# Two parity stores at the end of a row-normalizing kernel, and unshared buffers for its row sums

## Chip, cores, metric

One core of a Trainium2 chip. The metric is the device time of one execution in microseconds (us); medians of several executions are given.

## The reference

```python
x: [32, 512, 1024] float32          # 64 MiB in, 64 MiB out
sums = np.sum(np.abs(x), axis=-1, keepdims=True)
return (x / (sums + 1e-8)).astype(np.float32)
```

Each row of 1024 numbers is divided by the sum of its magnitudes. There is little arithmetic per byte: 134.22 MB cross between HBM and SBUF.

## The kernel before

The 16384 rows are cut into eleven tiles: ten of 12 rows per partition (6 MB), one of 8 (4 MB). Each tile is loaded by the SP queue, reduced and scaled in place by VectorE (DVE), with one row in twelve (five in the first tile, none at the end) left to ScalarE (ACT), and stored by the ACT queue. Four tile buffers rotate.

```python
    rows = [R] * ((per_partition - HEAD) // R + 2) + [HEAD - 2 * R]   # ten times 12, then 8
    sbuf = ctx.enter_context(tc.tile_pool(name="sbuf", bufs=BUFS))    # BUFS = 4
    stats = ctx.enter_context(tc.tile_pool(name="stats", bufs=4))
    # ... normalize():
        s = stats.tile([P, R], FP32)
        nc.vector.tensor_reduce(out=s[:, :k], in_=x_tile[...], ..., apply_absolute_value=True)
        nc.vector.tensor_scalar_add(out=s[:, :k], in0=s[:, :k], scalar1=EPS)
        inv = stats.tile([P, R], FP32)
        nc.vector.reciprocal(out=inv[:, :k], in_=s[:, :k])
        nc.vector.tensor_mul(out=x_tile[...], in0=x_tile[...], in1=inv[...])   # rows 0..kv
        # ... rows kv..k: nc.scalar.activation(Copy, scale=inv[:, r : r + 1])
    # ... the loop over the tiles:
            x_tile = sbuf.tile([P, R, d], FP32)
            nc.sync.dma_start(out=x_tile[:, :k, :], in_=piece(x_flat, i))
            normalize(...)
            nc.scalar.dma_start(out=piece(out_flat, i), in_=x_tile[:, :k, :])
```

## Time and profile before

| | before |
|---|---|
| median of the first 3 executions | 316.74 us (316.55 to 316.98) |
| span of the profiled execution (its time) | 317.3 us (318.93 us) |
| DVE busy | 268.7 us |
| DMA packets, bytes | 3168, 134.22 MB |

### The profile page before, as it was taken

The page shows a single profiled execution, that of the slowest core. Times are in us where ns is not written, and L with a number is a line of the kernel's source. Part 1 is how long each engine was busy: PE and PEld are TensorE (multiplying, and loading weights), DVE is VectorE, ACT ScalarE, POOL GpSimd, SP SyncE. Part 2 cuts the span into 40 slices and gives each one's busy share as a digit, 9 for nine tenths or more (in the row PEclk, how much of TensorE's full clock was granted, in tenths as well). Part 3 has the DMA queues.
Part 4 walks back from the last instruction along what each step waited for, and adds up shares of the span by engine and source line. Part 5 has one row for each costly group of instructions (what it writes and reads, how often), then busy time and mean ns, then how long its engine had stood idle before and what let it go on. Part 6 is the DMA issues. An engine that isn't in the chain of part 4 may idle for free.

```text
span 317.3 us, 170 instructions
## 1 busy us (share of the span) xinstructions
DVE 268.7 (85%) x44; ACT 13.5 (4%) x12; POOL 0.2 (0%) x4
## 2 busy tenths in 40 slices
DVE  0079999999999999989995996799699969999920
ACT  0010601001000000100100010000000000000000
POOL 0000000000000000000000000000000000000000
DMA  8999999999999999999999999999999999999994
GB/s 328 465 397 471 421 378 415 415 465 409 459 434 397 477 415 415 465 409 459 428 403 477 409 428 452 409 471 415 403 477 415 428 430 452 397 477 415 403 425 215
DMA packets 3168, 134.22 MB, mean 423 GB/s; under 512 B 352, under 2 KB 352, under 8 KB 352
## 3 DMA queue, kind: packets, MB, share of 16 engines
q1 hardware_dynamic: 1584, 67.11, 49.6%
q10 hardware_dynamic: 1584, 67.11, 48.9%
HBM read 67.11 MB, written 67.11 MB: 423 GB/s over the span
## 4 chain that ended last, share of the span: by engine, by line
DVE 52%; DMA 34%; another core or an unknown queue 9%; issue 0%; SPq 0%; DVEq 0%; ACTq 0%
DVE s L51 27%; DVE x_tile L61 24%; DMA x_tile<-in_x_dram 18%; DMA out_dram<-x_tile 16%; DVE inv L60 1%; DVE s L58 0%; SPq L78 0%; DVEq L60 0%; ACTq L85 0%
## 5 line engine op out<-in xcount | busy, mean ns | idle before, releaser
L51 DVE TENSOR_REDUCE s<-x_tile 128x12 f32<-128x12288 f32 (+1 forms) x11 | 138.2, 12561 | 32.9 <-DMA x_tile<-in_x_dram 32.9
L61 DVE TENSOR_TENSOR x_tile<-x_tile,inv 128x11264 f32<-128x11264 f32 (+3 forms) x11 | 126.5, 11504 | 0.4
L68 ACT ACTIVATE x_tile<-x_tile,inv 128x1024 f32<-128x1024 f32 x11 | 12.2, 1142 | 153.6 <-DVE inv L60 153.6
L60 DVE RECIPROCAL inv<-s 128x12 f32<-128x12 f32 (+1 forms) x11 | 2.5, 226 | 0.9
L58 DVE TENSOR_SCALAR s<-s 128x12 f32<-128x12 f32 (+1 forms) x11 | 1.9, 173 | 0.4
L68 ACT ACT_TABLE_LOAD x1 | 1.3, 1283 | 17.8 <-DMA x_tile<-in_x_dram 17.8
L100 POOL MEMSET const-bfloat16-1.0<- 128x1 bf16 x1 | 0.1, 102 | 0.0
L100 POOL MEMSET const-uint8-127<- 128x1 uint8 x1 | 0.1, 102 | 0.0
L100 POOL MEMSET const-float32-0.0<- 128x1 f32 x1 | 0.1, 99 | 0.2 <-issue 0.2
L100 POOL MEMSET const-float32-1.0<- 128x1 f32 x1 | 0.1, 99 | 0.0
## 6 DMA issues: line engine op xcount, KB each, us to landing
x_tile<-in_x_dram SPq DMA_DIRECT2D x10, 6144.0 KB, 39.2
out_dram<-x_tile ACTq DMA_DIRECT2D x10, 6144.0 KB, 43.7
x_tile<-in_x_dram SPq DMA_DIRECT2D x1, 4096.0 KB, 35.4
out_dram<-x_tile ACTq DMA_DIRECT2D x1, 4096.0 KB, 13.0
```

Of the source, the lines that this page charges most:

```text
L51: nc.vector.tensor_reduce(out=s[:, :k], in_=x_tile[:, r0 : r0 + k, :], axis=mybir.AxisListType.X, op=mybir.AluOpType.add, apply_absolute_v ...
L58: nc.vector.tensor_scalar_add(out=s[:, :k], in0=s[:, :k], scalar1=EPS)
L60: nc.vector.reciprocal(out=inv[:, :k], in_=s[:, :k])
L61: nc.vector.tensor_mul(out=x_tile[:, r0 : r0 + kv, :], in0=x_tile[:, r0 : r0 + kv, :], in1=inv[:, :kv].unsqueeze(2).to_broadcast([P, kv, d]),)
L68: nc.scalar.activation(out=row, in_=row, func=mybir.ActivationFunctionType.Copy, scale=inv[:, r : r + 1],)
L100: nc = _bacc.Bacc("TRN2", target_bir_lowering=False, num_devices=1)
```

## The change

Its intent, as far as it shows: finish the tail in smaller stores, and let no tile wait for the row sums of an earlier one.

```diff
-    stats = ctx.enter_context(tc.tile_pool(name="stats", bufs=4))
+    stats = ctx.enter_context(tc.tile_pool(name="stats", bufs=len(rows)))
...
-            nc.scalar.dma_start(out=piece(out_flat, i), in_=x_tile[:, :k, :])
+
+            parts = 1 if i + 2 < len(rows) else 2
+            for j in range(parts):
+                nc.scalar.dma_start(
+                    out=piece(out_flat, i)[j::parts, :, :], in_=x_tile[j::parts, :k, :]
+                )
```

"Parity store" below means such a pair: even partitions in one DMA, odd ones in the next.

## The prediction

"Unshared" is the outcome in which the packets of the tail keep their length, "shared" the one in which they take up to twice as long. The factor of two was a supposition; the 340 us follow from it and from the packet times measured in before (316.7 + 14.5 + 9.7 - 0.6). In before each DMA has 128 packets of data and 16 completions (22 x 144 = 3168 packets), and 32 KB in 1.213 us are 27.0 GB/s for an engine. No DMA there has 64 rows: that its packets would be dealt four to each of 16 engines was expected. The single long packets that the text tells of are 11 of 48 KB, of 1.85 to 2.53 us, between 129 and 248 us; 2.9 us is not among them.

> **What bounds the kernel now.** I read the page first: the DMA row of the slices beside the DVE row, then the queues and the chain, then the DMA issues, and last the tail by stretches.
>
> ```profile
> span 317.3 us, 170 instructions
> DVE 268.7 (85%) x44; ACT 13.5 (4%) x12; POOL 0.2 (0%) x4
> DVE  0079999999999999989995996799699969999920
> DMA  8999999999999999999999999999999999999994
> DMA packets 3168, 134.22 MB, mean 423 GB/s; under 512 B 352, under 2 KB 352, under 8 KB 352
> ...
> q1 hardware_dynamic: 1584, 67.11, 49.6%
> q10 hardware_dynamic: 1584, 67.11, 48.9%
> ...
> DVE 52%; DMA 34%; another core or an unknown queue 9%; issue 0%; SPq 0%; DVEq 0%; ACTq 0%
> ...
> out_dram<-x_tile ACTq DMA_DIRECT2D x10, 6144.0 KB, 43.7
> x_tile<-in_x_dram SPq DMA_DIRECT2D x1, 4096.0 KB, 35.4
> out_dram<-x_tile ACTq DMA_DIRECT2D x1, 4096.0 KB, 13.0
> ```
>
> DMA is at nine tenths or more in every slice but the first and last, while DVE has holes from the middle on. The two queues carry 98.5% of sixteen engines' span. The chain blames DVE for half of the span, but only because DVE's instructions happened to be the last link in each step. The bytes set the time: 134.22 MB at the rate of the middle of the kernel is 134.22/0.434 = 309 us, and the rest is start and end. The stretches show that rate and the tail:
>
> ```profile
> 120.00:220.00 100.00, 90.14 (x16) 3.44 (x3) 0.00 (x0) 1.00 1.00 434
> 220.00:283.00 63.00, 56.72 (x9) 0.00 (x0) 0.00 (x0) 1.00 0.99 429
> ...
> 289.00:303.00 14.00, 13.83 (x4) 0.00 (x0) 0.00 (x0) 1.00 0.96 414
> 303.00:314.00 11.00, 0.17 (x1) 0.00 (x0) 0.00 (x0) 1.00 0.91 392
> 314.00:317.30 3.30, 0.00 (x0) 0.00 (x0) 0.00 (x0) 1.00 0.02 10
> ```
>
> The last column is GB/s, the one before it the DMA share. After 283 us no load is left and stores alone still fill the engines; the last DVE instruction ends at 303.2 and the last store lands 13.0 us after its issue. That store is 128 packets of 32 KB, 8 on each of 16 engines; in the trace each takes 1.22 us, and a 48 KB packet of the earlier tiles takes 1.815 us. So 8 x 1.22 = 9.7 us of the 13.0 is transfer. The rest: 0.85 us pass between its issue and its first packet, and the engines don't finish together. Putting the packets end to end gives sixteen gapless rows. Of the sixteen completion events of the last store, thirteen lie between 314.13 and 314.29 and three at 314.84, 315.33 and 316.23. The latest engine has no gap anywhere in its tail, so it runs from its 48 KB packets straight into its 32 KB packets. Its lateness comes from single packets of 1.9 to 2.9 us scattered between 129 and 247 us. That one engine, not DVE and not the last issue, sets the end. The thirteen others idle 0.26 to 0.9 us near 304, waiting for the last issue.
>
> [...]
>
> **The change part by part.**
> The buffers: s and inv get 11 instead of 4, 7 x 2 x 48 B = 672 B more per partition. The ordering of waits shows what this does: from the fifth tile on, the reciprocal no longer waits for ACT, and the multiply of the same tile takes that wait over instead. So 7 extra waits on the DVE queue (21 ns each, about 70 ns between instructions instead of 25) move by one instruction and none vanishes: at most 7 x 0.05 = 0.35 us of DVE time, more likely 0. DVE already waits for loads in that half (1.14, 3.72, 4.31, 2.94 and 2.99 us before the reduces), which would swallow it. On the path: 0.
> The stores: two DMAs of 128 rows become four of 64. Bytes and packet sizes stay (a row is one packet either way); per engine 8 packets become 4 + 4. Added are 2 issues on ACT at 0.34 us, both while the first half is being moved; 2 x 16 completion packets of 9 ns, so 2 x 9 ns per engine; and one or two semaphores more at the closing wait, 0.05 us each by the spacing of such waits. The previous users of the extra completion semaphores landed long before (a store of about 218 us and loads already consumed), so no wait there. Perhaps the first packets start 0.1 to 0.3 us sooner[...]; thirteen engines would profit, the late one would not. Sum[...]: 316.7 + 0.0 (buffers) + 0.0 (issue) + 0.02 (completion packets) + 0.1 (closing waits) = about 316.8 us.
>
> **The rivals.**
> First, [...] every packet of the last two tiles takes up to twice as long: 8 x 1.815 = 14.5 us more for the 6 MB and 8 x 1.22 = 9.7 us more for the 4 MB, less the 0.6 us gap at 304: up to 340 us[...].[...]
> Second, a gain at the tail. If new DMAs rebalanced the engines, the 2 us by which one is late could go, to 314.7. Against: every engine still gets four and four packets, and the lateness is made before 250 us. Even with all of it and the 0.6 us gap gone, 314.1 is 0.8% down: faster by 2% (under 310.4) is below 309 + 2 of start + some of end, so as good as excluded.
> Third, the wait moved to the multiply delays the last store. 0.05 us; the late engine would not notice, since it has its previous packets until 306.
>
> **Range and chances.** It is one of two outcomes. Unshared: 316.8, spread 316.0 to 317.8 (three runs before span 0.43 us; the slow packets fall by chance). Shared: 325 to 340. I give the first two thirds[...], and the second one third[...]. Point 317.0, inside the likelier outcome. The range from 316.0 to 338.0 has to reach far into the second to hold 8 times in 10. Faster 0.01, within 2% 0.66, slower 0.33.
>
> **What would show it.** In the profile after: the stretches from 289 to 303 and 303 to 314 at 410 and 390 GB/s as before if unshared, near 220 if shared, with 48 KB packets of the last stores at 1.8 or up to 3.6 us. The issues must list four smaller stores, each on 16 engines. On DVE the queue's semaphore wait leaves the reciprocal and its multiply still has one, with holes before the reduces unchanged. The chain should still end in a store. I am wrong if the rate in the tail changes although packets keep their length (fewer than 16 engines), if time moves before 285 us, where the two kernels transfer the same, or if the late engines vanish.

## More of the kernel before

The prediction shows the lines on which its reading rests. Two more are needed for the part about buffers. They are from the page's groups of instructions: line, engine, operation, tiles and shapes, count, then busy time, mean duration in ns, and after the last bar the idle time of the engine just before them.

```profile
L61 DVE TENSOR_TENSOR x_tile<-x_tile,inv 128x11264 f32<-128x11264 f32 (+3 forms) x11 | 126.5, 11504 | 0.4
...
L60 DVE RECIPROCAL inv<-s 128x12 f32<-128x12 f32 (+1 forms) x11 | 2.5, 226 | 0.9
```

The small waits in front of reciprocals and multiplies come to 1.3 us in the whole kernel. That is what unshared buffers could remove at these two places.

## The result, and the profile after

The changed kernel took 317.03 us (median of 6, 316.57 to 318.47), the kernel before 316.70 us in 6 executions (316.55 to 316.98). The ratio is 1.0019, 95% interval 0.9995 to 1.0042: the same. A ratio here is the mean time of one kernel's fast runs over that of the other's of the same rounds (317.305/316.712), so it is not quite the ratio of the medians; those of the experiments are the record's and lie within 0.001 of the ratio of the means. The record calls everything under 2% "the same" (and a run whose interval crosses 2% "unclear"); where an interval below leaves out 1, I still take the difference for real.

The page of the kernel after: head, slices, packets, queues, and the DMA issues (tiles, queue, count, KB each, us from issue to landing).

```profile
span 315.0 us, 164 instructions
...
DVE  0079999999999999989995997799699969999920
...
DMA  8999999999999999999999999999999999999997
...
DMA packets 3200, 134.22 MB, mean 426 GB/s; under 512 B 384, under 2 KB 384, under 8 KB 384
...
q1 hardware_dynamic: 1584, 67.11, 49.9%
q10 hardware_dynamic: 1616, 67.11, 49.2%
...
out_dram<-x_tile ACTq DMA_DIRECT2D x9, 6144.0 KB, 46.1
out_dram<-x_tile ACTq DMA_DIRECT2D x2, 3072.0 KB, 17.5
...
out_dram<-x_tile ACTq DMA_DIRECT2D x2, 2048.0 KB, 10.6
```

The eleven stores have become nine, two and two. There are 32 packets more, two DMAs with 16 completions of 4 bytes each. Each smaller store runs on sixteen engines, four packets on each: in the trace the first half of the last tile begins with sixteen packets from 303.20 to 304.18 us, and its completions follow from 308.04 to 309.03, 4.84 us after each, four times 1.213. The bytes are the same, and the DMA row is full in all but the first and last slices, as before.

The stretches of the kernel after (us from the start, then DVE, ACT and POOL busy, clock, DMA share, GB/s), the same ones that the prediction shows of before:

```profile
220.00:283.00 63.00, 57.63 (x9) 0.00 (x0) 0.00 (x0) 1.00 1.00 432
...
289.00:303.00 14.00, 11.77 (x4) 0.00 (x0) 0.00 (x0) 1.00 1.01 435
303.00:314.00 11.00, 0.00 (x0) 0.00 (x0) 0.00 (x0) 1.00 0.88 381
```

435 and 381 GB/s stand where before had 414 and 392: nothing near 220, so the packets are not doubled. All but three of the 128 packets of 32 KB in the last tile take 1.213 us.

Why then is this span 2.3 us shorter than that of before, while the timed executions are the same? The trace does not name the engines, but a packet starts where the one before it on its engine ends (most within 4 ns; in 97% of the time from 50 to 283 us exactly sixteen are in transfer), and putting them end to end gives sixteen rows. In the trace of before one engine's last packet ended at 315.9 us and most others' at 313.8 to 313.9; after, all sixteen end between 312.9 and 313.9. The late engines of before are an accident of that execution. They show before the first split store, too, where both kernels transfer the same. The reduce of the last tile of 12 rows, first before, then after:

```profile
258.85 12.95 DVE L51 TENSOR_REDUCE s<-x_tile 128x12 f32<-128x12288 f32 x1 [2.99 <-DMA x_tile<-in_x_dram]
```

```profile
256.64 12.95 DVE L51 TENSOR_REDUCE s<-x_tile 128x12 f32<-128x12288 f32 x1 [2.52 <-DMA x_tile<-in_x_dram]
```

Of the sixteen completions of that tile's load, thirteen came by 254.6 us in before and three at 257.2, 257.7 and 258.8; after, they lie between 254.7 and 256.6.

The run with whole stores and new buffers (below) was profiled too, at 317.60 us, and its engines all end between 313.0 and 314.5 us: an engine 2 us late is no mark of whole stores. In 40 executions of the kernel before, over all the rounds, times lie between 316.51 and 320.14 us. Two single profiles do not compare here; the timed executions do.

The buffers did what the order of waits promised. The same two groups after, then the queue's own semaphore waits on these lines, from the views of the two source lines:

```profile
L61 DVE TENSOR_TENSOR x_tile<-x_tile,inv 128x11264 f32<-128x11264 f32 (+3 forms) x11 | 126.5, 11504 | 0.8
...
L60 DVE RECIPROCAL inv<-s 128x12 f32<-128x12 f32 (+1 forms) x11 | 2.5, 225 | 0.4
```

Before, at the reciprocal and at the multiply:

```profile
L60 DVEq EVENT_SEMAPHORE  x7: 21/21/21, 127.7 to 294.2; - x7
...
L61 DVEq EVENT_SEMAPHORE  x7: 21/21/21, 127.8 to 294.3; - x7
```

After, at the multiply alone:

```profile
L61 DVEq EVENT_SEMAPHORE  x7: 234/259/261, 127.6 to 292.0; - x7
```

The idle time moved from the reciprocal (0.9 to 0.4 us) to the multiply (0.4 to 0.8 us): 1.3 us became 1.2. The seven waits left over (234 to 261 ns) now span the reciprocal (202 to 229 ns) that they wait for.

### The profile page after: what moved, and what is told of

Its sections match the earlier page's. It is cut to its first block, busy times and chain, and to the rows that moved or that the text cites. A ratio compares the mean times of both kernels' runs of the same rounds, so it can differ in the third digit from the quotient of the medians.

```text
span 315.0 us, 164 instructions
## 1 busy us (share of the span) xinstructions
DVE 268.7 (85%) x44; ACT 13.5 (4%) x12; POOL 0.2 (0%) x4
## 4 chain that ended last, share of the span: by engine, by line
DVE 53%; DMA 33%; another core or an unknown queue 9%; issue 0%; SPq 0%; DVEq 0%; ACTq 0%
DVE s L51 27%; DVE x_tile L61 24%; DMA x_tile<-in_x_dram 17%; DMA out_dram<-x_tile 16%; DVE inv L60 1%; DVE s L58 0%; SPq L78 0%; DVEq L61 0%; ACTq L88 0%
```

## The experiments

Each run has before beside it on the same chip. The theory from the prediction: the sixteen DMA engines set the end, each needs the same packet times before and after, and neither part of the change touches them. The main rival: packets of the tail that take twice as long when a store is cut in two; this kernel escaped it, or it does not exist. Edits are against the changed kernel.

### The buffers alone

```diff
-            parts = 1 if i + 2 < len(rows) else 2
-            for j in range(parts): ...
+            nc.scalar.dma_start(out=piece(out_flat, i), in_=x_tile[:, :k, :])
```

> The change without its stores: eleven buffers for the row sums, whole stores. Theory A (both parts cost nothing, the 16 transfer engines set the end): 316.7 us, within 0.5 us of before; the wait on ACT leaves the reciprocal and sits at the multiply, holes of DVE before the reduces as before. Rival B (the buffers save DVE time and the split costs as much): under 316.2 us.

Measured: 316.69 us (6 executions, 316.59 to 317.60), before 317.35 us (11 executions, 316.51 to 319.04); ratio 0.9978 (0.9955 to 1.0002). The interval just includes 1, and before had several longer executions in these rounds (three above 318 us), so theory A holds within what this can resolve, though the medians lie 0.66 us apart and it had said 0.5; a gain of up to 0.45% is not excluded.

### The split alone

```diff
-    stats = ctx.enter_context(tc.tile_pool(name="stats", bufs=len(rows)))
+    stats = ctx.enter_context(tc.tile_pool(name="stats", bufs=4))
```

> The change without its buffers: the last two stores by parity, four buffers. Theory A: 316.7 to 317.0 us, 32 KB packets of the tail at 1.213 us. Rival B: over 317.3 us, or by theory C (the split makes single executions with a late engine more frequent) a median as before with single times above 318.

Measured: 317.63 us (316.40 to 317.93) against the same 317.35 us; ratio 0.9992 (0.9963 to 1.0021). The median itself falls in rival B's region, but so does before's; the ratio says that there is no cost. Two executions at 316.4 are as fast as any of before. The split does not make late engines more frequent in a way that can be seen (C): no execution passed 318, where before had three of eleven.

### Neighbouring halves instead of parity

The last two stores alone; the others stay whole. Two outcomes were expected, packets of twice the usual length and packets of the usual length.

```diff
+                for p in range(0, P, P // 2):
+                    nc.scalar.dma_start(
+                        out=piece(out_flat, i)[p : p + P // 2, :, :],
+                        in_=x_tile[p : p + P // 2, :k, :],
+                    )
```

> The last two stores as two DMAs of 64 neighbouring partitions each. [...] packets of the tail of about 2.4 and 3.6 us, 335 to 341 us, about +6 to +7%. [...] packets of 1.213 and 1.815 us, 316.7 to 317.2 us.[...]

Measured: 339.13 us (338.48 to 339.47), ratio 1.0678 (1.0648 to 1.0709). The same bytes, as many DMAs, as many rows in each, and 22 us more. The stretches of this kernel:

```profile
220.00:283.00 63.00, 57.61 (x10) 0.00 (x0) 0.00 (x0) 1.00 0.99 430
...
289.00:303.00 14.00, 11.23 (x4) 0.00 (x0) 0.00 (x0) 1.00 1.00 232
303.00:314.00 11.00, 0.00 (x0) 0.00 (x0) 0.00 (x0) 1.00 1.01 220
```

Until 283 us it is the same kernel; then the rate halves while the DMA share stays at 1.0. The engines are busy, on average at half speed. In the trace the 48 KB packets of the tail have a median of 3.83 us instead of 1.815, the 32 KB packets 2.37 instead of 1.213. Cutting a store into two DMAs of 64 rows can double the time of its packets, as the rival said, and parity avoids it. Why the halves are slow is not shown.

### Every fourth and every eighth partition

```diff
-            parts = 1 if i + 2 < len(rows) else 2
+            parts = 1 if i + 2 < len(rows) else 4      # the other run: 8
```

Is it the stride that helps? Theory P foretold that every fourth partition is as fast as whole stores and every eighth as slow as the halves. "Collide" in these texts means no more than that packets take longer than usual.

> The last two stores as four DMAs of every fourth partition (32 rows each).[...] Theory P[...]: packets of the tail of 1.21 and 1.81 us, 316.6 to 317.6 us. Theory Q (a smaller number of rows collides, whatever the stride): 325 us and more. Theory R (each DMA more costs 0.5 us, as 4.6 us for nine more splits in the run that split every store suggest): four DMAs more than the change, 319 us.

Measured: 317.40 us (316.95 to 317.81), before 317.59 us (316.54 to 318.07); ratio 0.9999 (0.9982 to 1.0016). All but a few packets are at 1.213 and 1.815 us (the 95th percentile too). P's numbers hold, Q and R fall. Its stretches:

```profile
289.00:303.00 14.00, 11.65 (x4) 0.00 (x0) 0.00 (x0) 1.00 0.97 421
303.00:314.00 11.00, 0.00 (x0) 0.00 (x0) 0.00 (x0) 1.00 0.89 381
```

> The last two stores as eight DMAs of every eighth partition (16 rows each): strided[...]. Theory P:[...] packets of about 3.6 and 2.4 us, 335 to 341 us as with neighbouring halves (339.1). Theory S (collisions come from neighbouring partitions and any stride avoids them): 316.6 to 319 us.

Measured: 338.79 us (338.23 to 339.38), ratio 1.0674 (1.0655 to 1.0692), within 0.4 us of the neighbouring halves. Its stretches:

```profile
289.00:303.00 14.00, 13.84 (x4) 0.00 (x0) 0.00 (x0) 1.00 1.10 267
303.00:314.00 11.00, 0.99 (x1) 0.00 (x0) 0.00 (x0) 1.00 0.94 213
```

Median packets are 3.75 and 2.30 us. Strided partitions can be as bad as neighbouring ones. S falls, P's numbers hold. For each store, eight DMAs of 16 rows are slow, four of 32 rows are free. (The store issues of this run took 2.3 us by the median of its 25, instead of 0.34, but with a DMA share of 1.10 and 0.94 the engines hardly waited for them; it is the packets that are long.) So of four ways of cutting two are free and two slow, and neither the number of DMAs (two: parity free, halves slow) nor their rows (64: the same two) nor their being strided (every fourth free, every eighth slow) sorts them by itself. What does is not shown. The cuts also differ in the HBM rows that a DMA writes; a run below that writes contiguous halves of HBM from parity partitions has store packets of 1.815 us in the median, beside loads, which speaks against HBM as the reason.

### Halves on two queues, and its control

Only the last store is cut; lower half on ACT, upper half on SP. Two outcomes were expected, up to 9.7 us more (the packets of the last store twice as long) and 317 to 320 us; that they hang on whether the engines stay in step is not shown.

```diff
+                for p, queue in ((0, nc.scalar), (P // 2, nc.sync)):
+                    queue.dma_start(
+                        out=piece(out_flat, i)[p : p + P // 2, :, :],
+                        in_=x_tile[p : p + P // 2, :k, :],
+                    )
```

> Only the last store (4 MB) in neighbouring halves, the lower issued by ACT, the upper by SP[...]. If the engines stay in step[...]: up to 9.7 us more, 325 to 327 us. If they fall out of step[...], the collisions go: 317 to 320 us.[...]

Measured: 317.74, 318.22, 324.38 and 326.53 us. The last two are over 1.5% above the fastest; their clock is 1.0 like the others'. The two fast ones are within the times of before (316.54 to 318.07) or just above. In the profiled execution (318.22) the median 32 KB packet took 1.213 us, but 24 of the 128 took over 1.3 us, the longest 2.44: some long packets, mostly none. The two slow executions were not profiled; why they are slow is not shown. The control cuts the same store by parity; the first outcome expected of it is that the spread belongs to the halves:

```diff
+                for j, queue in ((0, nc.scalar), (1, nc.sync)):
+                    queue.dma_start(
+                        out=piece(out_flat, i)[j::2, :, :], in_=x_tile[j::2, :k, :]
+                    )
```

> Control for the halves on two queues (317.7 to 326.5 us in four executions): only the last store cut, by parity, even on ACT and odd on SP. [...] every execution between 316.5 and 318.5 us, packets of 1.213 us. If two queues alone make it, single executions above 320 us.

Measured: 316.73 us (316.66 to 317.38), ratio 0.9985 (0.9940 to 1.0030). In its profile all 128 packets took at most 1.232 us, so the long packets of the profiled halves are not a matter of using two queues. Whether the wide spread comes from the halves too stays open, with four executions of each and the slow ones not profiled.

### Every store by parity, and the first nine alone

If one split is free, eleven should be.

```diff
-            parts = 1 if i + 2 < len(rows) else 2
+            parts = 2                                   # e4; in e8: 2 if i + 2 < len(rows) else 1
```

> Every store as two DMAs by parity, 22 instead of 13. It multiplies any cost of one split by 11/2: theory A (free): 316.7 to 317.5 us, nine more issues of 0.34 us hidden on ACT. If a split costs 0.15 us each (half of the 0.3 us that the medians differ by): 318 to 318.4 us.

Measured: 321.97 us (320.95 to 323.52), ratio 1.0141 (1.0111 to 1.0172). My expectation was wrong on both counts: 4.6 us more by the medians, not 0.8 nor 1.7.

> Parity split for the first nine stores, the last two whole: the complement of the change in place, and of the run that split every store (322.0 us). Theory T (a split costs only where loads run beside it, as longer packets near the start of a store): 320.5 to 322.5 us, long packets of 48 KB between 45 and 280 us on some engines as in that run. Theory U (the cost comes from 22 DMAs together, each equally): 9/11 of 4.6 us, about 320.7, which cannot be told from T here; a value within 0.5 us of before would say that the cost sits in the tail after all, against both.

Measured: 321.03 us (320.70 to 323.81), before 317.59; ratio 1.0140 (1.0106 to 1.0175). By the ratios the first nine splits alone cost as much as all eleven. With the split of the last two free, U falls (two of eleven equal shares would be 0.8 us, and the split alone allowed at most 0.7) and T holds: a parity store costs something while loads run beside it. Is it the number of DMAs?

### The first nine stores cut along the rows

```diff
+            step = k // 2 if i + 2 < len(rows) else k
+            for r in range(0, k, step):
+                nc.scalar.dma_start(
+                    out=piece(out_flat, i)[:, r : r + step, :], in_=x_tile[:, r : r + step, :]
+                )
```

> The first nine stores in two again, but cut along the rows in each partition (6 and 6), with all 128 partitions in each DMA: as many DMAs as in the run with the parity split of the first nine (321.0 us), packets of 24 KB. Theory V (each further store that begins beside loads costs about 0.4 us): 320 to 322 us. Theory W (the strided 64-row form costs, not the number): within 0.6 us of before. Smaller packets might add a little by themselves; at 9 ns for each of 18 x 8 it would be 0.7 us (an estimate from the 9 ns of a completion packet).

Measured: 317.02 us (316.88 to 317.96), before 317.18; ratio 0.9993 (0.9961 to 1.0025). As many DMAs, packets of 24 KB instead of 48 (2880 in the store queue instead of 1728), no cost. V falls, W holds. The same stretch, first of the parity cut and then of the row cut (the last column is GB/s):

```profile
220.00:283.00 63.00, 54.30 (x9) 0.00 (x0) 0.00 (x0) 1.00 1.01 426
```

```profile
220.00:283.00 63.00, 60.39 (x9) 0.00 (x0) 0.00 (x0) 1.00 1.01 434
```

### What makes the parity form cost beside loads

Two tries. The first leaves parity on the SBUF side only and writes contiguous halves in HBM. Its output is wrong, which doesn't matter for the time.

```diff
+            parts = 2 if i + 2 < len(rows) else 1
+            h = P // parts
-                    out=piece(out_flat, i)[j::parts, :, :], in_=x_tile[j::parts, :k, :]
+                    out=piece(out_flat, i)[j * h : (j + 1) * h, :, :], in_=x_tile[j::parts, :k, :]
```

> Wrong result on purpose (rows land in a permuted place): the first nine stores by parity on the SBUF side, to two contiguous halves of the piece in HBM. It asks which side makes the parity cut cost 3.4 to 4.4 us beside loads (321.0 us), where a cut along the rows costs nothing (317.0). HBM side (every second 48 KB row written): 316.6 to 317.8 us. SBUF or engine side: 320 to 323 us as before.

Measured: 323.26 us (322.29 to 323.84), ratio 1.0174 (1.0127 to 1.0221). Writing every second row of HBM is not the cause. The time is even 2 us above that of the parity form and just over the 320 to 323 us expected; why is open.

The second cuts all loads by parity too, beside the first nine stores.

```diff
-            nc.sync.dma_start(out=x_tile[:, :k, :], in_=piece(x_flat, i))
+            for j in range(2):
+                nc.sync.dma_start(
+                    out=x_tile[j::2, :k, :], in_=piece(x_flat, i)[j::2, :, :]
+                )
```

> First nine stores and all loads by parity, correct result. If the cost beside loads comes from loads of 128 rows and stores of 64 rows[...], it goes when both are dealt alike: 316.6 to 318 us. If the 64-row form itself costs beside other traffic: 321 us and more, as twice as many such transfers run.

Measured: 320.51 us, single executions 320.98, 320.69, 318.19 and 320.32; ratio 1.0073 (1.0021 to 1.0125). Neither expectation is met. What the traces say is in this table. A long packet is one over 30 ns above the usual time for its size, counted between 50 and 283 us, with the engines found as above. The times are of the profiled execution.

| kernel | long packets: loads / stores | their excess, us: sum / worst engine | last data or completion packet ends, us | time, us |
|---|---|---|---|---|
| before | 13 / 0 | 3.9 / 1.9 | 315.9 | 318.93 |
| after | 0 / 0 | 0 / 0 | 313.9 | 316.81 |
| first nine by rows | 51 / 0 | 7.2 / 1.1 | 314.8 | 317.96 |
| all by parity | 59 / 73 | 30.6 / 5.2 | 318.5 | 321.54 |
| first nine by parity | 75 / 74 | 33.9 / 4.3 | 317.7 | 320.84 |
| same, HBM in halves | 79 / 51 | 40.2 / 5.8 | 320.7 | 323.84 |
| same, loads by parity too | 34 / 1 | 8.9 / 4.3 | 317.9 | 320.98 |

First, in every row the time is the last packet's end plus 2.9 to 3.2 us: the latest engine sets the time, across a range of 7 us. Second, parity stores beside whole loads bring some 130 to 150 long packets where the others have 0 to 51, and in this stretch long packets of stores appear nowhere else, but for a single one in the last row. Long packets of loads alone say less: the profiles of the buffers alone and the split alone, where all stores up to 283 us are whole, have 39 and 42 of them, 8.9 and 9.6 us in sum, against 17 to 31 us of excess on loads in the three rows of parity stores beside whole loads. Third, with loads cut alike the stores' long packets are gone (74 to 1), as the first expectation wants, but two engines still fall behind: they end at 316.3 and 317.9 us, the others by 314.3. Whether those two have the same cause is open: the run also changed when loads are issued.

## Why the prediction was right

**The bound.** It named the engines' packet times and the latest engine as what sets the end. The table bears this out in seven kernels.

**The buffers: 0 us.** Right; alone they gave 0.9978, within noise. The wait moved to the multiply as foreseen. One detail was off: the queue's separate semaphore waits halved from 14 to 7, where the prediction had none vanish. It was worth 0.1 us of DVE idle time that DVE did not need. The bound was a little low too: a wait makes the gap between two instructions 0.10 us instead of 0.034, so seven are 0.5 us and not 0.35.

**The stores: 0.1 us.** Right: the split alone gave 0.9992, and even eight DMAs in place of two (every fourth partition) gave 0.9999. Whether the first packets would start 0.1 to 0.3 us sooner can't be seen, as the engines of after were still busy at the issue.

**The rival with doubled packets.** Its size was right (340 us at most; the halves took 339.1 and every eighth partition 338.8), and it did not apply to parity. No run shows why it comes true for some cuts and not for others. The reason for giving it only a third was poor: it would have held for the neighbouring halves as well, and these cost 22 us. So that the outcome with two thirds was the right one is in part luck.

**The late engine.** The prediction read one late engine as the state of the kernel and said it would be wrong if late engines vanished. They did vanish from the profile after, but not because of the change: the kernel before, to go by its times (316.51 to 320.14 us), has executions with and without them. The second sign of being wrong came true as well: time did move before 285 us, by 2.2 us at the reduce shown above, with the same cause. These tests were badly chosen; one profile cannot carry them. And the chain could not tell whether it "still ends in a store": in both profiles its last piece is DVE's multiply (to 303.2 and 300.9 us). The gap near 304 us (0.40 to 0.75 us by the rows, not 0.26 to 0.9) belonged to the same execution: after, the last DVE instruction ended at 300.9 us, and the engines had no gap.

**Range.** 316.0 to 338.0 us was so wide because the doubling of packets could not be decided from the profile of before. The halves and the strides decided it afterwards.

## What to carry to other kernels

Where every DMA engine is full, as here, splitting a transfer at the end gained nothing; read the trace for the latest engine, and compare timed executions rather than two profiles. If partitions must be split, measure the way of cutting: here parity or every fourth partition was free in the tail (317.0 us against 316.7, 317.4 against 317.6), neighbouring halves or every eighth doubled the packet time (medians of 3.83 and 3.75 us instead of 1.815 for 48 KB). Where loads run beside the stores, cut along the rows inside the partitions: here the parity cut cost 1.4% (321.0 us), the row cut nothing (317.0 us).
